# One plain feed-forward chunk instead of two at the start of each block, with the next two chunks' first products moved in between

## The chip, the cores and the metric

One core of a Trainium2 chip. The metric is the device time of one execution in microseconds (us), the median over runs. TensorE (PE in the profile) multiplies matrices and writes to eight PSUM banks; VectorE (DVE) and ScalarE (ACT) do elementwise work and read PSUM; GpSimd (POOL) issues accumulating transfers here; SyncE (SP) issues the weight loads.

## The reference

The trunk has two layers over 512 and 256 tokens of 1024 features, in float32. Each layer is feed-forward, mixer, feed-forward, so there are four feed-forward blocks, f0 to f3, each with its own weights:

```python
def swiglu_ffn(x, w1, w2):
    gate, up = jnp.split(x @ w1, 2, axis=-1)
    return (jax.nn.silu(gate) * up) @ w2
...
x = x + 0.5 * swiglu_ffn(rmsnorm(x, norm_g[li, 0]), ffn_w1[li, 0], ffn_w2[li, 0])
h = rmsnorm(x, norm_g[li, 1])
...
x = x + mix
x = x + 0.5 * swiglu_ffn(rmsnorm(x, norm_g[li, 2]), ffn_w1[li, 1], ffn_w2[li, 1])
```

The first mixer is a gated linear recurrence, the second windowed attention; a last RMSNorm closes the trunk. The hidden width is 2816, 22 chunks of 128.

## The kernel before

All 768 tokens are worked on at once, features on the partitions, tokens in two halves of 384 (half 0, half 1). Every float32 operand is split into a rounded high part and the rest (`split`: a ScalarE cast, then a VectorE subtraction), and a product is three matmuls: high x high, high x low, low x high.

**A chunk** is one 128-wide piece of the hidden layer, gate and up. It is computed in one of two ways.

- *Plain* (`up_plain`): for each half of the tokens, gate and up are each 8 blocks of 128 input features times three matmuls (L288 to L290). A plain chunk needs the activations as they are: b00 and b10 are the first and second 512 features of half 0, b01 and b11 those of half 1.
- *Seven products* (`up_pair`, matmuls on L527): gate/up and the two halves of the features form a 2 x 2 block matrix of weights, features and token halves one of activations, and seven products of sums (p1 to p7) take the place of eight. Four are of single blocks or of sums on the weights' side with b00, b10, b11 (p1, p2, p3) and the others use sums of activation blocks, t1 to t4 (p5 with t1, p6 with t2, p7 with t3, p4 with t4). The products are added up in four PSUM banks a, b, c, d; some banks are read in between: L544 copies p1 out of a before p2 is added to it, L550 copies p7 out of c before p4 is added, L556 reads p5 in d before p3 is added.

The weights' sums come in three ways: loads with an accumulating transfer on GpSimd's queue (`into`: the gate/up sum of the lower block, and `s3` for p7), and two VectorE additions (L243) before p6 and p3 in the order `UP`. Each product's weights are split into a buffer of their own (L229, L230); a plain operand takes two buffers (L186, L189). There are 8 such buffers (`WBUFS`) and 4 for unsplit loads (`RAWBUFS`). `done` gives a buffer back and `ahead` stages the next weights as far as there is room, in the order in which the products use them.

**The opening of a block.** The activations come out of the last stage token block by token block: normalised (L351), transposed on TensorE (L411, `turn`), copied (L414), split (L293, L294). Half 0 is ready first. `turn` for half 1 and `sums`, which forms t1 to t4 with four subtractions for each 512 features (L441, L442, L444, L445) and splits them, are deferred: `run_later` calls in the plain chunks issue them one by one. Before the change there are two plain chunks: both chunks' half 0, then both chunks' half 1, then the first seven-product chunks.

```python
PLAIN = 2
UP = ("p1", "p7", "p2", "p5", "p4", "p6", "p3")
```

**Groups.** Four chunks make a group of hidden activations. Their blocks are put together (`put`, `gather`, with `mix` for the sums) as operands of the seven-product down projection (`down_quad`, L608), whose results VectorE adds to x (L671). There are five groups; the last two chunks of a block go through a plain down projection.

**Order.** A framework queues the instructions of each engine, not strictly in the order of the code: one that waits may be overtaken by a later one of the same engine that does not depend on it. On the chip each queue is fixed. `issue_after` forces an order in a queue.

Of the kernel before, what the change touches and what calls it, by code (L numbers as in the profile page):

```python
# [12 lines left out]
AF = mybir.ActivationFunctionType  # L13
# [3 lines left out]
P = 128  # L17
D = 1024
DFF = 2816
NC = D // P  # L20
NF = DFF // P
# [13 lines left out]
SEQS = ((0, TA), (TA, TB))  # L35
H = T // 2
HB = H // P
PLAIN = 2
GROUPS = (NF - PLAIN) // 4
WBUFS = 8  # L40
RAWBUFS = 4
SLOTS = 21
RING = 1024
WARM = 21
UP = ("p1", "p7", "p2", "p5", "p4", "p6", "p3")
DOWN = ("p1", "p2", "p5", "p4", "p7", "p6", "p3")
FACTOR = {"p1": "b00", "p2": "b10", "p3": "b11", "p4": "t4", "p5": "t1", "p6": "t2", "p7": "t3"}


class Trunk:  # L50
# [104 lines left out]
    def load_next(self):  # L155
        key, srcs, shape, how = self.queue.pop(0)
        raws = []
        first = len(srcs) // 2 if len(srcs) == 4 else 0
        for src in srcs[first:] + srcs[:first]:
            t = self.wp.tile([P, 1024], F32, tag="wr", name=self.name("wr"), bufs=RAWBUFS)  # L160
            raw = t[:, : shape[0] * shape[1]].rearrange("p (a b) -> p a b", a=shape[0])
            if len(srcs) < 4:
                src = src.rearrange("(k p) c -> p k c", p=P)
            self.last_load = self.nc.sync.dma_start(raw, src)
            raws.append(raw)
        raws = raws[len(raws) - first :] + raws[: len(raws) - first]
        if len(raws) == 1:
            steps = self.plain_steps(key, raws[0], shape)
        else:
            steps = self.quad_steps(key, raws, srcs, how)  # L170
        self.loaded.append((len(raws), steps))

    def wtile(self):
        return self.wp.tile([P, 1024], F32R, tag="w", name=self.name("w"), bufs=WBUFS)
# [24 lines left out]
    def quad_steps(self, key, raws, srcs, order):  # L199
        nc = self.nc  # L200
        flat = lambda t: t.rearrange("p a b -> p (a b)")
        up = len(raws) == 2
        if up:
            a11, a12, a21, a22 = (flat(t[:, h : h + 4, :]) for t in raws for h in (0, 4))
            three = [srcs[1].rearrange("(k p) c -> p k c", p=P)[:, :4, :]]
        else:
            a11, a12, a21, a22 = (flat(t) for t in raws)
            three = [srcs[2][:, i : i + 1, :] for i in range(2)]
        s3 = []
        if not up:  # L210
            self.into(a21, a22)
        for i, src in enumerate(three):
            t = self.wp.tile([P, 512], F32, tag="s3", name=self.name("s3"), bufs=2)
            self.last_load = nc.sync.dma_start(t.rearrange("p (a b) -> p a b", a=src.shape[1]), src)
            self.into(t, a11[:, i * 512 : (i + 1) * 512])
            s3.append(t)
        if up:
            self.into(a21, a22)

        def split(name, srcs):  # L220
            if up:
                w = self.wtile()
                hi, lo = w[:, :512], w[:, 512:]
            else:
                hi, lo = self.wtile(), self.wtile()
            n = srcs[0].shape[-1]
            for i, src in enumerate(srcs):
                h, l = (t[:, i * n : (i + 1) * n] for t in (hi, lo))
                nc.scalar.copy(h, src)  # L229
                low = nc.vector.tensor_sub(l, src, h.bitcast(F32)).ins  # L230
            view = lambda t: t.rearrange("p (a b) -> p a b", a=4 if up else 2)
            self.staged[(*key, name)] = (view(hi), view(lo), 1 if up else 2)
            return low

        own = {"p1": [a11], "p2": [a12], "p3": [a12], "p4": [a22], "p5": [a21], "p6": [a11], "p7": s3}
        sums = {"p6": (a11, a21), "p3": (a12, a11)}
        last = [None]

        def step(name):
            if name in sums:  # L240
                into, term = sums[name]
                with self.tc.issue_after(last[0]):
                    nc.vector.tensor_add(into, into, term)  # L243
            last[0] = split(name, own[name])
            if up and name == "p5":
                self.halved = self.halved or last[0]

        return [(1 if up else 2, lambda name=name: step(name)) for name in order]
# [209 lines left out]

    xn = [None] * NBLK
    normed = mixed = first = halved = None  # L460
    normal = None
    plains = 0

    def after_block(self, b, row):
# [11 lines left out]
    def plan_ffn(self, tag, w1, w2):  # L476
        def up(i):
            gate, up = (w1[:, c * P : (c + 1) * P] for c in (i, NF + i))
            if i < PLAIN:
                self.plan((tag, i, 0), gate, (NC, P))  # L480
                self.plan((tag, i, 1), up, (NC, P))
            else:
                self.plan_quad((tag, i), (gate, up), (NC, P), UP)

        for g in range(GROUPS):
            for i in range(4 * g, 4 * g + 4):
                up(i)
            self.plan_down((tag, "down", g), w2[4 * g * P : (4 * g + 4) * P, :])
        for i in range(NF - 2, NF):
            up(i)  # L490
        for c in range(2):
            self.plan((tag, "last", c), w2[(NF - 2) * P :, c * 512 : (c + 1) * 512], (2, 512))
# [6 lines left out]
    def up_plain(self, tag, j, half):  # L499
        pss = []  # L500
        for c in range(2):
            wh, wl = self.take((tag, j, c))
            ps = self.ps(H)
            for k in range(NC):
                b = self.operand(f"b{k // 4}{half}", k % 4)
                self.mm3(ps, (wh[:, k, :], wl[:, k, :]), b, k == 0, k == NC - 1)
                if self.first:
                    self.first()
                    self.first = None
                if half == 0 and k in (((), (2, 6)), ((3, 7), (3, 7)))[j][c]:  # L510
                    self.run_later()
            if half:
                self.done((tag, j, c))
            pss.append(ps)
        t = self.tmp(H)
        with self.tc.issue_after(self.normed) if self.normed else nullcontext():
            self.nc.scalar.activation(t, pss[0], AF.Silu)
        self.normed = None
        self.nc.vector.tensor_mul(t, t, pss[1])
        return t  # L520
# [15 lines left out]
    def up_pair(self, tag, j, hold=False):  # L536
        nc = self.nc
        key = (tag, j)
        a, b, c, d = (self.ps(H) for _ in range(4))
        v, w, t = (self.tmp(H) for _ in range(3))  # L540
# [35 lines left out]
        else:  # L576
            finish()
        free("p3")
        yield w

    def down_quad(self, tag, g, hid):
# [91 lines left out]
    def ffn(self, tag, next_row):  # L673
        for g in range(GROUPS):
            hid = {}

            def put(name, src, kp):
                if name not in hid:
                    hid[name] = self.big([P, 2, 2, H], F32R)
                return self.split(src, hid[name][:, kp, 0, :], hid[name][:, kp, 1, :])  # L680

            def gather(ts, kp):
                self.mix(ts[0], ts[1], ts[2], ts[3], lambda name, src: put(name, src, kp))

            if g == 0:
                ts = {}
                for half in range(2):
                    for j in range(PLAIN):
                        t = ts[2 * j + half] = self.up_plain(tag, j, half)
                        name = f"b{j}{half}"  # L690
                        if name != "b01":
                            low = put(name, t, 0)
                        if name == "b00" and self.whole:
                            with self.tc.issue_after(low):
                                for parts in self.whole[:2]:
                                    self.nc.vector.tensor_add(*parts)
                            del self.whole[:2]
                gather(ts, 0)
                self.run_later(len(self.deferred))
            for kp in range(2):  # L700
                if g == 0 and kp == 0:
                    continue
                ts = []
                for j in range(2):
                    for half, t in enumerate(self.up_pair(tag, 4 * g + 2 * kp + j, j == 0)):
                        ts.append(t)
                        name = f"b{j}{half}"
                        if name != "b01":
                            put(name, t, kp)
                gather(ts, kp)  # L710
            self.down_quad(tag, g, hid)
# [646 lines left out]
class Unit:  # L1358
# [220 lines left out]
```

## Time and profile before

| | |
|---|---|
| median of three runs | 2731.8 us (2731.26 to 2732.34) |
| span of the profiled execution | 2730.5 us |
| outside the span, against the median | 1.3 us |
| TensorE busy | 2720.2 us, 100% |
| VectorE busy | 2110.3 us, 77% |
| ScalarE busy | 1339.0 us, 49% |
| GpSimd busy | 204.8 us, 7% |
| transfers | 293.98 MB, 108 GB/s |

The profile is of one execution, whose own total is not listed apart from its span. Engine busy times are those with at least one instruction in flight; matmuls overlap, so TensorE counts as busy although each matmul lasts 334 ns and the next starts after about half of that. A row of a group reads: line, engine, operation, output and inputs with partitions x elements, count, then busy us and mean ns of one, then idle time of the engine just before them and what ended it. In the chain, a row is start, length and what ran. In the windows a row is a stretch of the span with each engine's busy us and its instructions in brackets, the granted TensorE clock, the share of the transfer engines, and GB/s. In a timeline a row is start, length, engine, line, operation, count.

### The profile page before, as it was taken

Reading aid. Unit: us, or ns where it says so; the run is one execution under the profiler, and the core shown is the slowest. Engines: PE = TensorE matmul, PEld = TensorE weight load, DVE = VectorE, ACT = ScalarE, POOL = GpSimd, SP = SyncE. Lnnn points to the kernel's source line nnn. Section 1 sums busy time; section 2 is a strip of 40 time slices with the busy share of each in tenths; the row PEclk is TensorE's granted clock in tenths of the full one; section 3 lists DMA queues with packets and bytes.
Section 4 is the critical chain, followed back from the end, with each engine's and each line's share of the span. In section 5 each row is a group of like instructions: output and inputs, shape, how many; then the busy total and the mean of one; then the engine's idle time right before and its main releaser. Section 6 shows DMA issues by size and latency. Waiting matters only on the chain.

```text
span 2730.5 us, 44549 instructions
## 1 busy us (share of the span) xinstructions
PE 2720.2 (100%) x17305; PEld 2483.8 (91%) x17305; DVE 2110.3 (77%) x3789; ACT 1339.0 (49%) x2507; POOL 204.8 (7%) x243
## 2 busy tenths in 40 slices
PE   9999999999999999999999999999999999999998
PEld 9999999889888889999999999999987789999998
DVE  8888788567476778778888878887847768787877
ACT  6444444456466554444446444444546754444443
POOL 1110110000000000111110011101000000111000
PEclk9999999999999999999999999999999999999999
DMA  6544554311110524465553355544422123555443
GB/s 183 136 123 117 127 143 120 123 56 48 55 41 25 143 65 120 113 147 129 128 121 102 88 129 139 135 116 112 133 72 78 47 62 87 130 139 135 117 112 108
DMA packets 331411, 293.98 MB, mean 108 GB/s; under 512 B 11752, under 2 KB 258240, under 8 KB 331200
## 3 DMA queue, kind: packets, MB, share of 16 engines
q1 hardware_dynamic: 294352, 212.89, 26.6%
q0 software_dynamic: 32544, 64.76, 13.6%
q10 hardware_dynamic: 4304, 13.49, 1.4%
q8 instruction: 135, 2.21, 0.3%
q14 instruction: 76, 0.62, 0.1%
HBM read 216.91 MB, written 9.44 MB: 83 GB/s over the span
## 4 chain that ended last, share of the span: by engine, by line
PE 97%; DVE 1%; ACT 1%; issue 0%; DMA 0%; DVEq 0%; SPq 0%; ACTq 0%
PE ps L527 42%; PE ps L608 21%; PE ps L288 9%; PE ps L289 9%; PE ps L290 9%; PE ps L856 1%; PE ps L643 1%; PE ps L1451 1%; PE ps L1442 1%; PE ps L1004 1%; PE ps L1390 1%; PE ps L411 1%; PE ps L980 0%; PE ps L969 0%; DVE x L671 0%
## 5 line engine op out<-in xcount | busy, mean ns | idle before, releaser
L527 PE MATMUL ps<-big,w 128*128 128x384 f32 x6720 | 1169.7, 334 | 0.6 <-ACT tA L544 0.6
L527 PEld LDWEIGHTS ps<-big,w 128*128 128x128 f32 x6720 | 1165.9, 188 | 2.8 <-ACT tA L544 1.2
L229 ACT CAST w<-wr 128x512 fp32r<-128x512 f32 (+1 forms) x606 | 424.2, 710 | 721.8 <-DVE wr L243 305.4
L230 DVE TENSOR_TENSOR w<-wr,w 128x512 fp32r<-128x512 f32 (+1 forms) x606 | 480.5, 798 | 225.4 <-ACT w L229 158.5
L608 PE MATMUL ps<-w,big 128*128 128x512 f32 x2520 | 575.4, 389 | 0.0
L608 PEld LDWEIGHTS ps<-w,big 128*128 128x128 f32 x2520 | 472.8, 188 | 97.5 <-DVE x L671 0.3
L671 DVE SCALAR_TENSOR_TENSOR x<-ps,x 128x512 f32<-128x512 f32 x468 | 302.6, 681 | 4.7 <-PE ps L290 4.7
L288 PE MATMUL ps<-w,big 128*128 128x512 f32 x576 | 232.5, 404 | 0.0
L290 PE MATMUL ps<-w,big 128*128 128x512 f32 x576 | 225.5, 391 | 0.0
L289 PE MATMUL ps<-w,big 128*128 128x512 f32 x576 | 225.1, 391 | 0.0
L288 PE MATMUL ps<-big,w 128*128 128x384 f32 (+2 forms) x640 | 217.9, 342 | 0.2
L289 PE MATMUL ps<-big,w 128*128 128x384 f32 (+2 forms) x640 | 215.8, 337 | 0.4 <-DVE big L371 0.2
L290 PE MATMUL ps<-big,w 128*128 128x384 f32 (+2 forms) x640 | 215.1, 336 | 0.0
L293 ACT CAST big<-tA 128x384 fp32r<-128x384 f32 x296 | 147.8, 512 | 117.5 <-DVE tA L572 40.4
L153 POOL DMA_DIRECT2D s<-wr x122 | 106.3, 913 | 1300.1 <-DMA wr<-in_ffn_w_dram 623.6
L189 DVE TENSOR_TENSOR w<-wr,w 128x1024 fp32r<-128x1024 f32 (+1 forms) x88 | 105.9, 1209 | 82.0 <-ACT w L186 73.4
L294 DVE TENSOR_TENSOR big<-tA,big 128x384 fp32r<-128x384 f32 x296 | 159.9, 551 | 8.2 <-ACT big L293 7.8
L153 POOL DMA_DIRECT2D wr<-wr x101 | 87.6, 868 | 1009.3 <-DVE tA L1110 386.0
L186 ACT CAST w<-wr 128x1024 fp32r<-128x1024 f32 (+1 forms) x90 | 93.0, 1035 | 93.4 <-PE ps L289 66.3
L288 PEld LDWEIGHTS ps<-w,big 128*128 128x128 f32 x576 | 108.3, 188 | 25.6 <-issue 4.6
L290 PEld LDWEIGHTS ps<-w,big 128*128 128x128 f32 x576 | 108.1, 188 | 23.5 <-issue 0.4
L289 PEld LDWEIGHTS ps<-big,w 128*128 128x128 f32 x640 | 121.0, 189 | 9.4 <-DVE big L294 1.0
(191 smaller groups left out, 2891.8 us busy)
## 6 DMA issues: line engine op xcount, KB each, us to landing
wr<-in_ffn_w_dram SPq DMA_DIRECT2D x264, 512.0 KB, 3.9
s<-wr POOLq DMA_DIRECT2D x122, 256.0 KB, 5.1
s<-in_ffn_w_dram SPq DMA_DIRECT2D x120, 256.0 KB, 3.3
wr<-wr POOLq DMA_DIRECT2D x80, 256.0 KB, 4.2
wr<-in_hg_w_in_dram SPq DMA_DIRECT2D x40, 512.0 KB, 3.8
wr<-wr POOLq DMA_DIRECT2D x21, 512.0 KB, 6.0
spill<-x ACTq DMA_DIRECT2D x12, 512.0 KB, 2.9
x<-spill ACTq DMA_DIRECT2D x12, 512.0 KB, 3.3
```

What stands on the lines that cost most here:

```text
L153: self.nc.gpsimd.dma_start(out, src, accum_op=ALU.add)
L189: eng.tensor_sub(lo, raw[:, ks, :], hi.bitcast(F32))
L229: nc.scalar.copy(h, src)
L230: low = nc.vector.tensor_sub(l, src, h.bitcast(F32)).ins
L288: nc.tensor.matmul(out, a[0], b[0], start=first, stop=False)
L289: nc.tensor.matmul(out, a[0], b[1], start=False, stop=False)
L290: nc.tensor.matmul(out, a[1], b[0], start=False, stop=last)
L293: self.nc.scalar.copy(hi, src)
L294: return self.nc.vector.tensor_sub(lo, src, hi.bitcast(F32)).ins
L527: self.nc.tensor.matmul(ps, a[x], b[y], start=first and k == 0 and i == 0, stop=k == 3 and i == 2, skip_group_check=True,)
L608: nc.tensor.matmul(ps, a[x], w[y], start=name == chain and kp == 0 and q == 0, stop=kp == 1 and q == 2, skip_group_check=True,)
L671: return self.nc.vector.scalar_tensor_tensor(x, ps, c, x, ALU.mult, ALU.add).ins
```

## The change

One chunk per block is plain, not two. Chunks 1 and 2 are now of the seven-product kind, in a new function `open_pair` whose weights are ordered by `OPEN`. Chunk 0's half 0 is followed by p1 and p2 of chunk 1 and of chunk 2, which need only half 0; then come chunk 0's half 1, p3 of both, p5 of both, and then the rest of chunk 1 (p7, p4, p6) and of chunk 2. Chunk 3 follows in `up_pair` as before. The deferred steps for half 1 are issued behind the same number of matmuls as before. The first gather of four blocks now takes place behind chunk 1's products. In `OPEN` both VectorE additions of a chunk's weights come before p3.

```diff
-PLAIN = 2
-GROUPS = (NF - PLAIN) // 4
+GROUPS = (NF - 2) // 4
...
+OPEN = ("p1", "p2", "p3", "p5", "p7", "p4", "p6")
@@ load_next
-        self.loaded.append((len(raws), steps))
+        if how is not OPEN:
+            self.loaded.append((len(raws), steps))
+        elif self.opened is None:
+            self.loaded.append((2, steps[:2]))
+            self.opened = steps[2:]
+        else:
+            a, b = self.opened, steps[2:]
+            self.loaded.append((0, steps[:2]))
+            self.loaded.append((2, [a[0], b[0], a[1], b[1]] + a[2:]))
+            self.loaded.append((2, b[2:]))
+            self.opened = None
@@ quad_steps
-        sums = {"p6": (a11, a21), "p3": (a12, a11)}
+        sums = {"p6": [(a11, a21)], "p3": [(a12, a11)]}
+        if order is OPEN:
+            sums = {"p3": sums["p6"] + sums["p3"]}
...
-            if name in sums:
-                into, term = sums[name]
+            for into, term in sums.get(name, ()):
@@ plan_ffn
-            if i < PLAIN:
+            if i == 0:
...
-                self.plan_quad((tag, i), (gate, up), (NC, P), UP)
+                self.plan_quad((tag, i), (gate, up), (NC, P), OPEN if i < 3 else UP)
@@ up_plain
-                if half == 0 and k in (((), (2, 6)), ((3, 7), (3, 7)))[j][c]:
+                if half == 0 and c and k in (2, 6):
                     self.run_later()
@@ new
+    def open_pair(self, tag, j, hold):
...
+        p("p1", a, True, False)
+        nc.scalar.copy(v, a)
+        free("p1")
+        self.run_later()
+        p("p2", a, False, True)
+        nc.scalar.activation(a, a, AF.Silu)
+        free("p2")
+        self.run_later()
+        yield
+        d = self.ps(H)
+        p("p3", d, True, False)
+        nc.scalar.copy(w, d)
+        free("p3")
+        yield
+        p("p5", d, False, True)
+        free("p5")
+        yield
+        c, b = self.ps(H), self.ps(H)
+        p("p7", c, True, False)
+        nc.vector.tensor_add(w, w, c)
+        free("p7")
+        p("p4", c, False, True)
+        nc.vector.tensor_sub(w, w, d)
+        free("p4")
+        p("p6", b, True, True)
+        t = self.tmp(H)
+        nc.vector.tensor_sub(v, v, b)
+        nc.vector.tensor_sub(t, c, v)
+        nc.vector.tensor_mul(t, t, a)
+        free("p6")
+        yield t
+        nc.vector.tensor_sub(w, w, v)
+        nc.vector.tensor_add(v, v, d)
...
@@ ffn
             if g == 0:
-                ts = {}
-                for half in range(2):
-                    for j in range(PLAIN):
-                        t = ts[2 * j + half] = self.up_plain(tag, j, half)
...
-                gather(ts, 0)
+                first = [self.up_plain(tag, 0, 0)]
+                low = put("b00", first[0], 0)
...
+                for j in (1, 2):
+                    pairs[j] = self.open_pair(tag, j, j == 2)
+                    next(pairs[j])
+                first.append(self.up_plain(tag, 0, 1))
                 self.run_later(len(self.deferred))
+                for _ in range(2):
+                    for j in (1, 2):
+                        next(pairs[j])
+                pairs[0] = first
```

More of the change, by code (lines that the diff above doesn't have):

```diff
@@ L460 @@
     normed = mixed = first = halved = None
-    normal = None
+    normal = opened = None
     plains = 0
@@ L578, in up_pair, with finish @@
         free("p3")
+        yield w
+    def open_pair(self, tag, j, hold):
+        nc = self.nc
+        key = (tag, j)
+        a, d, c, b = self.ps(H), None, None, None
+        v, w = (self.tmp(H) for _ in range(2))
+        p = lambda name, ps, first, last: self.product(key, name, FACTOR[name], ps, first, last)
+        free = lambda *names: [self.done((*key, name)) for name in names]
+        p("p1", a, True, False)
[31 more added lines that the diff above has]
+        nc.vector.tensor_add(v, v, d)
+        def finish(after=None):
+            with self.tc.issue_after(after) if after else nullcontext():
+                self.last_act = nc.scalar.activation(v, v, AF.Silu).ins
+            self.last_dve = nc.vector.tensor_mul(w, v, w).ins
+        if hold:
+            self.tail = finish
+        else:
+            finish()
         yield w
@@ L683, in gather @@
                 self.mix(ts[0], ts[1], ts[2], ts[3], lambda name, src: put(name, src, kp))
+            pairs = {}
             if g == 0:
-                ts = {}
-                for half in range(2):
-                    for j in range(PLAIN):
-                        t = ts[2 * j + half] = self.up_plain(tag, j, half)
[L690 to L697, printed above, removed]
-                gather(ts, 0)
+                first = [self.up_plain(tag, 0, 0)]
+                low = put("b00", first[0], 0)
+                if self.whole:
+                    with self.tc.issue_after(low):
+                        for parts in self.whole[:2]:
+                            self.nc.vector.tensor_add(*parts)
+                    del self.whole[:2]
+                for j in (1, 2):
+                    pairs[j] = self.open_pair(tag, j, j == 2)
+                    next(pairs[j])
+                first.append(self.up_plain(tag, 0, 1))
                 self.run_later(len(self.deferred))
+                for _ in range(2):
+                    for j in (1, 2):
+                        next(pairs[j])
+                pairs[0] = first
             for kp in range(2):
-                if g == 0 and kp == 0:
-                    continue
                 ts = []
                 for j in range(2):
-                    for half, t in enumerate(self.up_pair(tag, 4 * g + 2 * kp + j, j == 0)):
+                    n = 4 * g + 2 * kp + j
+                    for half, t in enumerate(pairs.get(n) or self.up_pair(tag, n, j == 0)):
                         ts.append(t)
                         name = f"b{j}{half}"
-                        if name != "b01":
+                        if name != "b01" and (n or half):
                             put(name, t, kp)
```

## The prediction

> **What bounds the kernel now.** I read the page first: busy times, the clock row, the chain that ended last. Then the groups by shape, the chain in order of time, and the windows and timelines of the four openings of a feed-forward block (f0 to f3), the only places that the diff touches.
>
> ```profile
> span 2730.5 us, 44549 instructions
> ...
> PE 2720.2 (100%) x17305; PEld 2483.8 (91%) x17305; DVE 2110.3 (77%) x3789; ACT 1339.0 (49%) x2507; POOL 204.8 (7%) x243
> ...
> PEclk9999999999999999999999999999999999999999
> ...
> PE 97%; DVE 1%; ACT 1%; issue 0%; DMA 0%; DVEq 0%; SPq 0%; ACTq 0%
> ```
>
> TensorE is the bound: it carries 97% of the chain, and only 10.3 us of the span have no matmul in flight. The median of the runs, 2731.8, is 1.3 us above the profiled span. What lies outside the span stays as it is, so the sum is a difference taken off 2731.8. Anything between 2726.3 and 2737.3 (0.2%) I call no change.
>
> ```profile
> 48.51 29.12 PE ps L527 x168
> ...
> 1031.07 29.12 PE ps L527 x168
> 1060.19 28.60 PE ps L608 x126
> 1088.79 58.26 PE ps L527 x336
> ...
> 1521.03 29.12 PE ps L527 x168
> ...
> 2272.23 29.12 PE ps L527 x168
> ```
>
> These pieces of the chain give the pace: 58.26/336 = 0.1734 us per matmul of 384 columns, without a hole. The four x168 pieces are the first two seven-product chunks of f0, f1, f2 and f3. Their starts, which I call S, are 48.51, 1031.07, 1521.03 and 2272.23.
>
> **The change part by part.**
>
> *Matmuls.* A plain chunk is 2 halves x 2 (gate, up) x 8 k x 3 = 96 matmuls, a seven-product chunk 7 x 4 x 3 = 84. One chunk per block changes kind: 12 x 0.1734 = 2.08 us less TensorE work per block, 8.32 us in four, with as many weight loads less. All of it is on the path, so the best case is 2731.8 - 8.3 = 2723.5.
>
> *Order.* After 48 plain matmuls on half 0 come p1, p2 of both chunks (48), the plain half 1 (48), p3 of both (24), p5 of both (24), then p7. So p7, the first user of t3, starts at S exactly as the old first p1 did. But p5 needs t1 24 matmuls (4.16 us) before S, and its weights and p3's must be staged 4.2 to 8.3 us before S, where formerly the first split chunk needed nothing before S.
>
> *VectorE work.*
>
> ```profile
> L230 DVE TENSOR_TENSOR w<-wr,w 128x512 fp32r<-128x512 f32 x480 | 326.7, 686 | 148.2 <-ACT w L229 142.5
> L189 DVE TENSOR_TENSOR w<-wr,w 128x1024 fp32r<-128x1024 f32 x86 | 104.6, 1221 | 82.0 <-ACT w L186 73.4 <-PE ps L527 7.5
> L243 DVE TENSOR_TENSOR wr<-wr,wr 128x512 f32<-128x512 f32 x80 | 54.6, 683 | 0.0
> L556 DVE TENSOR_TENSOR tA<-tA,ps 128x384 f32<-128x384 f32 x80 | 44.1, 551 | 26.6 <-PE ps L527 26.5
> L544 ACT COPY tA<-ps 128x384 f32<-128x384 f32 x80 | 38.4, 479 | 59.7 <-PE ps L527 59.4
> ```
> ```profile
> 28.61 1.89 DVE L590 TENSOR_TENSOR x<-x,x 128x512 f32<-128x512 f32 x3
> ...
> 46.32 0.68 DVE L230 TENSOR_TENSOR w<-wr,w 128x512 fp32r<-128x512 f32 x1
> 46.92 0.68 DVE L230 TENSOR_TENSOR w<-s,w 128x512 fp32r<-128x512 f32 x1
> 47.52 2.69 DVE L294 TENSOR_TENSOR big<-big,big 128x768 fp32r<-128x768 f32 x3
> 50.13 0.55 DVE L294 TENSOR_TENSOR big<-tA,big 128x384 fp32r<-128x384 f32 x1
> 50.60 1.29 DVE L230 TENSOR_TENSOR w<-wr,w 128x512 fp32r<-128x512 f32 x2
> ```
>
> Back to back, VectorE starts a 512-wide weight operation every 0.60 us (46.32 to 46.92), a 768-wide one every (50.13 - 47.52)/3 = 0.87, a 384-wide one every 0.47 (50.13 to 50.60). Per block the change adds 7 splits and 2 sums of weights (9 x 0.60 = 5.4) and 7 operations on products (3.3); it removes two 1024-wide weight splits (about 1.2 each) and two multiplications (0.94). Net +5.4 us, while the time in which to do it shrinks by 2.08.
>
> ```profile
> core 0: us, PE busy (x) PEld busy (x) DVE busy (x) ACT busy (x) POOL busy (x), PEclk, DMA share, GB/s
> 15.67:33.90 18.23, 18.23 (x114) 17.99 (x114) 16.95 (x26) 14.32 (x26) 6.34 (x7) 1.00 1.11 254
> 33.90:50.13 16.23, 16.23 (x96) 16.23 (x95) 15.65 (x20) 10.07 (x16) 0.86 (x1) 1.00 0.21 45
> 50.13:77.63 27.50, 27.50 (x160) 27.50 (x159) 24.30 (x44) 14.88 (x26) 2.62 (x3) 1.00 0.50 125
> 994.27:1008.83 14.56, 14.47 (x92) 13.83 (x91) 11.37 (x14) 14.54 (x25) 1.72 (x2) 1.00 0.46 109
> 1008.83:1026.01 17.18, 17.18 (x101) 17.18 (x100) 17.06 (x24) 10.57 (x18) 0.00 (x0) 1.00 0.05 16
> 1031.07:1060.19 29.12, 29.12 (x170) 29.12 (x169) 21.59 (x36) 14.54 (x25) 2.63 (x3) 1.00 0.42 109
> 1498.78:1515.29 16.51, 16.51 (x97) 16.51 (x96) 16.51 (x23) 10.59 (x18) 0.00 (x0) 1.00 0.05 17
> 2249.99:2267.16 17.17, 17.17 (x101) 17.17 (x100) 17.05 (x23) 10.57 (x18) 0.00 (x0) 1.00 0.05 16
> ```
>
> The rows 33.90:50.13, 1008.83:1026.01, 1498.78:1515.29 and 2249.99:2267.16 run from the first subtraction of the sums (t1 to t4 of both halves of the first 1024 features) to their last split. In each VectorE is full. These ends lie 5.06, 5.74 and 5.07 us before S in f1, f2, f3, and 1.62 us *behind* S in f0, where the normalisation of the first tokens starts everything later.
>
> *f1 to f3.* The sums are 16 operations of 0.87 = 13.9 us. What else must be through before p7 can finish: the first plain product's multiplication and split and the second's multiplication (1.4), five weight splits (two p3, two p5, one p7: 3.0), and p3's four sums (2.4). Together 20.7 us from 1008.83, so 1029.5, 1.5 us before S; 3.9 before if the four sums go into the 3.2 us in which VectorE was idle in 994.27:1008.83. The p3 splits are due 6 to 8 us before S: the old sums held 3.3 us of foreign operations between their own, so there is room. I take a stall of 0 here; ends 0 and 2.1.
>
> *f0.* Again 13.9, with p3's sums and splits (2 x 1.8), two p5 and one p7 (1.8) and one multiplication (0.47). The first p3's 1.8 can take the place of the three x21 subtractions at 28.61, which nobody needs before the down products at 77.63. That leaves 18.0 from 33.90: 51.9 for the last split (t2), 51.0 for the one before (t3). p7's second half is due at S + 1.04 = 49.55: 1.5 us late. If the first p3 also comes behind 33.90 it is 3.3; if p6's first half (6 matmuls, 1.04) fills the hole, 0.4. I take 1.5.
>
> *Behind S.* In f1 VectorE has 7.5 us idle from S to the down products, in f0 3.2. In f0 what does not fit (about 1 us) eats into the down weights staged ahead; a down product lasts 28.60/7 = 4.09 us, so a delay of 1 us is hidden. Cost 0, upper end 2.
>
> *Banks read between two products.* p2 adds to the bank from which p1's copy (L544) has yet to be read, and p4 to the one that w's addition (as L556) reads; before, another product always lay between, now none does in the code. p3 and p5 are covered by the other chunk's.
>
> ```profile
> PE ps L527 <- ACT tA L544: 0.6, 1, 0.6
> ```
> ```profile
> 998.30 0.34 PE L290 MATMUL ps<-big,w 128*128 128x384 f32 x1
> 998.48 0.93 PE L411 MATMUL ps<-ident_r,big 128*128 128x128 f32 x7
> ```
> ```profile
> 1000.31 1.83 DVE L294 TENSOR_TENSOR big<-big,big 128x768 fp32r<-128x768 f32 x2
> ```
>
> The first row is the one time that TensorE waited for that copy: 0.6 us. The others show that the queue's order isn't the code's: TensorE had run 24 matmuls of the plain chunk by 998.48, before b10 was split (1000.31). In the code gate's 13th matmul needs b10, so the 24 are the b00 halves of gate and up, and transposes of the other half fill on. In the same way p1 of the other chunk can go between p1 and p2, and p6 between p7 and p4. I charge one uncovered turnaround in all, 0.6; ends 0 and 16 x 0.6 = 9.6. The Trainium skill ("TensorE: Matmul & The Clock Gate", "Step-by-step: what each phase is for") says that only weight loads are pulled ahead and matmuls stay in the order in which they were queued; by that rule alone nothing on the chip fills such a wait, and the sum would come out at the upper end. Whether it is paid hangs on the order that was queued, and these rows speak for a filled one.
>
> *Others.* ScalarE gets 7 casts, 2 copies and 2 Silu for 2 casts and 2 Silu; outside its full stretch 994.27:1008.83 it has a third idle: 0, up to 1. SP and POOL: one more load (256 KB) and two accumulating transfers per block, at a DMA share of 0.05 to 0.5; in f0 (1.11 until 33.90) they come 20 us before use: 0, up to 1. The third chunk's loads go out some 15 us later, and still some 15 us ahead of use: 0.
>
> *Sum.* -8.3 + 1.5 (f0) + 0.6 = -6.2: 2725.6.
>
> **The rivals.** (A) The forecast, f0 losing most of its gain, 2724.5 to 2727.5. (B) All four blocks gain: 2723.5. For: the filled holes above; against: f0's sums end behind S already. (C) Slower: the turnarounds aren't filled, and p4's wait on VectorE stands behind the sums in its queue. Per opening 2 x 0.6 for ScalarE and 2 x (0.6 + 1.3, half of a batch of three splits, 2.6) = 5.0, against 2.08: +2.9 x 4, 2743.5. It decides from 2.08 us per opening, and shows as slower from 3.45. For: VectorE full in all four rows; against: the reordering. (D) VectorE is late in all openings: p3's sums, asked for ahead of t1 to t4, push these back by 1.5 to 2.1 us beyond my count, and the gain is gone: 2729.5 to 2732. Against: 1.5 to 3.9 us of slack in f1 to f3. (E) f0's stall is long enough to lower TensorE's clock: at half pace the 36 matmuls of p7, p4 and p6 cost 6.2 more, 2731.8. The clock row shows no such fall anywhere. The same page (its Part 1) has the clock halve after an idle window of about 3.4 us; no hole of that length between matmuls is in the quoted rows.
>
> **How the numbers follow.** A 0.44, B 0.19, D 0.20, E 0.04, C 0.13. Faster: B and all but 0.04 of A, 0.59; same: that 0.04, D and E, 0.28; slower: C, 0.13. The range runs from B's 2723.0 (half a microsecond of scatter) to D's end, 2731.5; C and a corner of D lie outside. A alone: 2724.5 to 2727.5.
>
> **What would show it.** 384 matmuls fewer in the 384-column groups of L288 to L290, 336 more in L527's; the stretch from the first plain matmul to the first down product shorter by 2.1 us in f1 to f3, and by 0 to 1.5 in f0, with TensorE waiting there for the split of t3 or for p7's weights. Wrong if TensorE waits for L544's successor or for w's addition in every opening (C), or for L230 in f1 to f3 (D).

## The result, and the profile after

| | before | after |
|---|---|---|
| median | 2732.1 us (2731.3 to 2733.5) | 2761.3 us (2759.5 to 2762.0) |
| ratio | | 1.0105 [1.0091, 1.0119] |
| span of the profiled execution | 2730.5 us | 2760.0 us |
| TensorE busy | 2720.2 us | 2724.4 us |
| time without a matmul in flight | 10.3 us | 35.6 us |

The change makes the kernel 29 us slower, 1.1%. The page of the kernel after, with the span, the busy times, the chain by engine and the costliest group:

```profile
span 2760.0 us, 44576 instructions
...
PE 2724.4 (99%) x17257; PEld 2481.1 (90%) x17257; DVE 2131.2 (77%) x3845; ACT 1349.3 (49%) x2535; POOL 211.1 (8%) x251
...
PE 92%; DVE 3%; DMA 2%; ACT 2%; issue 1%; POOL 0%; DVEq 0%; SPq 0%; ACTq 0%; POOLq 0%
...
L538 PE MATMUL ps<-big,w 128*128 128x384 f32 x7056 | 1238.8, 335 | 19.9 <-DVE tA L618 17.7
```

There are 48 matmuls fewer (17257 for 17305), as the change says, 8.3 us at 0.1734 us each. Yet TensorE is busy 4.2 us longer, and its share of the chain fell from 97% to 92%. Both halves of the loss are to be explained: 25.3 us more idle, and busy time that is 12.5 us above what 48 matmuls fewer should have left (4.2 up where 8.3 down was due). A stretch in which no matmul is in flight is called a hole below.

Line numbers moved by about ten: the product matmul L527 is now L538, the weight cast and split L229 and L230 are L239 and L240, the weights' sum L243 is L254, the operand split L294 is L305, the down product L608 is L671 and its addition to x L734. L618 is new, `w += c` in `open_pair`: it reads p7 out of bank c before p4 may add to it. The list of TensorE's waits (total, times, longest) names the place:

```profile
PE ps L538 <- DVE tA L618: 17.7, 5, 6.7
PE ps L300 <- DVE big L305: 4.7, 3, 4.2
...
PE ps L538 <- DVE big L305: 0.5, 1, 0.5
```

p4 waits for L618 in every block, 17.7 us in all. The chain in order of time tells the blocks apart; these rows start the second group behind each opening, first before, then after:

```profile
193.24 58.26 PE ps L527 x336
...
1175.66 58.26 PE ps L527 x336
...
1665.62 58.26 PE ps L527 x336
...
2416.82 58.26 PE ps L527 x336
```
```profile
208.80 58.26 PE ps L538 x336
...
1194.66 58.26 PE ps L538 x336
...
1690.07 58.26 PE ps L538 x336
...
2446.27 58.26 PE ps L538 x336
```

The lead of before grows by 15.6 us in f0, 3.4 in f1, 5.5 in f2 and 5.0 in f3, together 29.5, the whole difference of the spans. Behind the openings the pace is the old one, 58.26 us for 336.

**Where f1's 3.1 us hole comes from.** Timelines of f1, each row with the idle time before it and what ended it; first the load of chunk 3's weights and its accumulating transfer before the change, then the way from that load to TensorE after it:

```profile
997.05 2.11 SPq L164 DMA_DIRECT2D wr<-in_ffn_w_dram  x2
...
1001.63 0.86 POOL L153 DMA_DIRECT2D s<-wr  x1 [17.33 <-DMA wr<-in_ffn_w_dram]
```
```profile
1043.86 3.19 SPq L164 DMA_DIRECT2D wr<-in_ffn_w_dram  x4
...
1048.59 0.89 POOL L153 DMA_DIRECT2D s<-wr  x1 [48.60 <-DMA wr<-in_ffn_w_dram]
...
1054.36 0.62 ACT L239 CAST w<-s 128x512 fp32r<-128x512 f32 x1 [5.71 <-DMA s<-wr]
...
1055.01 0.69 DVE L240 TENSOR_TENSOR w<-s,w 128x512 fp32r<-128x512 f32 x1 [4.21 <-ACT w L239]
...
1060.51 0.54 DVE L618 TENSOR_TENSOR tA<-tA,ps 128x384 f32<-128x384 f32 x1
...
1061.11 2.20 PE L538 MATMUL ps<-big,w 128*128 128x384 f32 x11 [3.09 <-DVE tA L618]
```

Chunks 1 and 2 are now both in work from before half 1 until their last product, and hold all four raw buffers. Chunk 3's loads go out at 1043.86, where before they had gone out at 997.05: 46.8 us later, or 31 without the 15.6 us that f0 had lost by then. GpSimd then adds to s, ScalarE waits 5.71 us for that transfer, VectorE 4.21 us for ScalarE. The transfer itself landed 5.6 us after its issue, and four weight loads had gone out in the 5 us before it; before the change the same transfer took 3.3 us (in f2 and f3 it took 6.5 and 6.7 us, for 4.4 and 4.2). In VectorE's fixed queue chunk 3's splits stand ahead of chunk 2's L618 (1060.51), so a product of chunk 2 waits for weights of chunk 3. Chunk 3's own first product comes only behind this hole, 17 us after its loads went out. The 3.09 us are what TensorE could not fill.

**f0's other hole.** Two pieces of the chain, and then timelines of f0:

```profile
21.25 7.41 DMA s<-wr
61.46 8.12 DMA s<-wr
```
```profile
28.74 0.69 DVE L254 TENSOR_TENSOR wr<-wr,wr 128x512 f32<-128x512 f32 x1 [4.85 <-DMA s<-wr]
...
32.76 1.82 DVE L305 TENSOR_TENSOR big<-big,big 128x768 fp32r<-128x768 f32 x2
...
33.77 0.69 PE L300 MATMUL ps<-big,w 128*128 128x384 f32 x1 [4.23 <-DVE big L305]
```

p3's sum now comes first and adds into a11, in place. The accumulating transfer issued at 21.25 still reads a11, until 28.66. VectorE stands there for 4.85 us with the split of b01 (32.76) behind it, and TensorE stands for 4.23. The second piece (61.46) is chunk 3's late s, as in f1, and makes the 6.7 us hole.

**What a hole costs besides itself.** The granted clock is the share of full speed at which TensorE may run. Four microseconds behind each of the five longest holes (windows: TensorE busy and matmuls, then the granted clock):

```profile
1061.11:1065.11 4.00, 4.00 (x23) 1.00 0.35 114
1554.91:1558.91 4.00, 4.00 (x15) 0.63 0.33 123
2312.43:2316.43 4.00, 4.00 (x15) 0.60 0.34 116
72.66:76.66 4.00, 4.00 (x13) 0.52 0.63 128
33.77:37.77 4.00, 4.00 (x13) 0.50 0.01 1
```

Behind four of the five the clock was about half, and 13 or 15 matmuls ran where 23 run at full clock. That is 8 + 8 + 10 + 10 = 36 matmuls, 6.2 us: half of the 12.5 us of busy time. One of the four half-clock stretches runs on behind its window. Counted over the whole trace from the starts of consecutive matmuls, each against the usual distance for its shape (173 ns for 384 columns), the half clock cost 7.4 us. The same count puts the other 5 us into pauses that do not show as idle: a wait counts as idle only once the last matmul, 334 ns long, has ended, and a pause shorter than that leaves TensorE busy.

### The profile page after: what moved, and what is told of

The parts are those of the page before. It is cut to its first block, busy times and chain, and to the rows that moved or that the text cites. A ratio compares the mean times of both kernels' runs of the same rounds, so it can differ in the third digit from the quotient of the medians.

```text
span 2760.0 us, 44576 instructions
## 1 busy us (share of the span) xinstructions
PE 2724.4 (99%) x17257; PEld 2481.1 (90%) x17257; DVE 2131.2 (77%) x3845; ACT 1349.3 (49%) x2535; POOL 211.1 (8%) x251
## 4 chain that ended last, share of the span: by engine, by line
PE 92%; DVE 3%; DMA 2%; ACT 2%; issue 1%; POOL 0%; DVEq 0%; SPq 0%; ACTq 0%; POOLq 0%
PE ps L538 41%; PE ps L671 20%; PE ps L299 8%; PE ps L300 8%; PE ps L301 8%; PE ps L921 1%; DMA s<-wr 1%; PE ps L706 1%; PE ps L1516 1%; PE ps L1507 1%; DMA wr<-in_ffn_w_dram 1%; PE ps L1069 1%; PE ps L1455 1%; DVE w L240 1%; ACT w L239 0%
## 5 line engine op out<-in xcount | busy, mean ns | idle before, releaser
L538 PE MATMUL ps<-big,w 128*128 128x384 f32 x7056 | 1238.8, 335 | 19.9 <-DVE tA L618 17.7
L538 PEld LDWEIGHTS ps<-big,w 128*128 128x128 f32 x7056 | 1228.1, 188 | 27.2 <-DVE tA L618 19.6
L239 ACT CAST w<-wr 128x512 fp32r<-128x512 f32 (+1 forms) x630 | 439.2, 707 | 708.6 <-DVE wr L254 317.0
L240 DVE TENSOR_TENSOR w<-wr,w 128x512 fp32r<-128x512 f32 (+1 forms) x630 | 496.0, 793 | 217.6 <-ACT w L239 153.8
L671 PE MATMUL ps<-w,big 128*128 128x512 f32 x2520 | 576.5, 389 | 0.8 <-DVE x L734 0.8
L671 PEld LDWEIGHTS ps<-w,big 128*128 128x128 f32 x2520 | 472.4, 188 | 99.4 <-ACT big L304 1.4
L734 DVE SCALAR_TENSOR_TENSOR x<-ps,x 128x512 f32<-128x512 f32 x468 | 302.6, 681 | 4.8 <-PE ps L301 4.7
L300 PE MATMUL ps<-big,w 128*128 128x256 f32 (+2 forms) x512 | 174.0, 340 | 5.1 <-DVE big L305 4.7
L299 PE MATMUL ps<-big,w 128*128 128x256 f32 (+2 forms) x512 | 175.7, 346 | 0.1
L301 PE MATMUL ps<-big,w 128*128 128x256 f32 (+2 forms) x512 | 173.0, 338 | 0.0
L305 DVE TENSOR_TENSOR big<-tA,big 128x384 fp32r<-128x384 f32 x296 | 159.7, 551 | 6.7 <-ACT big L304 6.5
L199 DVE TENSOR_TENSOR w<-wr,w 128x1024 fp32r<-128x1024 f32 (+1 forms) x80 | 96.2, 1208 | 81.7 <-ACT w L196 73.4
L299 PEld LDWEIGHTS ps<-w,big 128*128 128x128 f32 x576 | 108.3, 188 | 25.7 <-issue 4.6
L196 ACT CAST w<-wr 128x1024 fp32r<-128x1024 f32 (+1 forms) x82 | 84.5, 1034 | 92.0 <-PE ps L300 66.3
L301 PEld LDWEIGHTS ps<-w,big 128*128 128x128 f32 x576 | 108.1, 188 | 23.6 <-issue 0.4
L300 PEld LDWEIGHTS ps<-w,big 128*128 128x128 f32 x576 | 108.4, 188 | 19.6
```

The source lines that it names most:

```text
L199: eng.tensor_sub(lo, raw[:, ks, :], hi.bitcast(F32))
L299: nc.tensor.matmul(out, a[0], b[0], start=first, stop=False)
L300: nc.tensor.matmul(out, a[0], b[1], start=False, stop=False)
L301: nc.tensor.matmul(out, a[1], b[0], start=False, stop=last)
L305: return self.nc.vector.tensor_sub(lo, src, hi.bitcast(F32)).ins
L538: self.nc.tensor.matmul(ps, a[x], b[y], start=first and k == 0 and i == 0, stop=k == 3 and i == 2, skip_group_check=True,)
```

## The experiments

Theories. L: chunk 3's weights arrive too late, since its loads wait for raw buffers. Q: the arrival is harmless by itself, and only the order of VectorE's queue makes p4 wait. W: in f0 the in-place sum of p3 waits for the accumulating transfer. All medians stand beside the kernel before on the same chip (2732.2 to 2732.6).

**Chunk 3's staging behind chunk 2's L618 (for Q).**

```diff
+        if self.held + ... > WBUFS or (self.shut and self.loaded[0][1] is self.third):
...
+        with self.tc.issue_after(self.behind) if steps is self.third and self.behind else nullcontext():
+            go()
@@ open_pair
+        summed = nc.vector.tensor_add(w, w, c).ins
+        if hold:
+            self.shut, self.behind = False, summed
```

> The splits of chunk 3's weights are queued on VectorE behind the addition of chunk 2's p7 to w, which p4 waits for; loads, buffers and products stay as in the changed kernel. Theory Q (queue order): in the changed kernel VectorE stood before chunk 3's p7 weights, whose accumulating transfer had not landed, and so delayed an addition that TensorE was waiting for. Expected by Q: the four waits of TensorE on that addition (6.7, 3.1, 3.7 and 4.0 us, 17.7 in all with a short one) go, with the half-clock stretch that followed the longest (about 2 us) and small waits behind it: 2761.3 - 20 = 2738 to 2743; a wait of about 4 us in f0's first half stays. Rival L (the loads themselves come too late for TensorE): the wait only moves to chunk 3's p1 or p7, less than a third is won, 2754 or more. Rival B (VectorE has too much work): the waits shrink by less than half, 2750 to 2758.

Measured: 2753.3 us, 1.0075 [1.0060, 1.0090], 8 us better than the change. TensorE's waits:

```profile
PE ps L542 <- DVE w L242: 5.0, 5, 3.2
PE ps L303 <- DVE big L308: 4.2, 3, 3.8
PE ps L542 <- ACT w L241: 2.2, 3, 1.0
PE ps L677 <- DVE w L242: 2.1, 1, 2.1
```

The wait on L618 is gone, and TensorE's products wait for their weights themselves (L241, L242) instead; the last row is the same for a down product. Q's 2738 to 2743 is missed by 10 us. The queue's order was the place of the wait and a part of its size; the late weights stay.

**p3's sums in another order (for W): a12 += a11, then a12 += a21, so that a11 is not written before p6.**

```diff
-            sums = {"p3": sums["p6"] + sums["p3"]}
+            sums["p3"].append((a12, a21))
```

> p3's weights in the opening chunks are summed as a12 += a11, then a12 += a21, so that a11 isn't overwritten before p6; one VectorE addition more per chunk. Theory W: in f0 the in-place sum into a11 had to wait until the accumulating transfer that reads a11 had landed (7.4 us behind a transfer of x on GpSimd's queue), and VectorE stood before it with the split of b01 behind; TensorE then waited 4.2 us and ran at a granted clock of 0.5 for 4.9 us. Expected by W: f0 shorter by 4.2 + 2.4 = 6.6, the rest as it was or up to 1 longer: 2754 to 2757. Rival: f0's first half waits because VectorE is simply full; then no gain, 2760 to 2763.

Measured: 2764.6 us, 1.0117 [1.0100, 1.0134]: a miss, 3 us worse. A timeline of f0 and the waits:

```profile
27.98 0.62 ACT L239 CAST w<-wr 128x512 fp32r<-128x512 f32 x1 [3.65 <-DVE wr L254]
...
29.13 0.55 PE L422 MATMUL ps<-ident_r,big 128*128 128x128 f32 x3 [2.07 <-ACT big L425]
```
```profile
PE ps L538 <- DVE tA L618: 19.3, 4, 5.8
```

The 4.2 us hole went, but p3's cast in ScalarE's queue still waited 3.65 us for the sums, ahead of the turned operands' copies. In f1 to f3 the holes at L618 were 2.7, 1.3 and 0.8 us longer than in the change, and the transfer of s ahead of them took 3.3, 1.0 and 0.6 us longer from issue to landing (8.9, 7.5 and 7.3 us). Why it did is not shown.

**Both together.**

> e1's queue order and e2's order of sums together. Q and W: their gains add up, 20 + 6.6 us: 2733 to 2737, no stretch at half clock left in f0, the blocks f1 to f3 within 1 us of the kernel before. If my count of the freed matmuls were the whole of it, all four blocks would be 2.1 us shorter than before, 2724; I expect f0 to keep 3 to 5 us of short waits, as its sums end behind the first use. Rival L: 2745 or more.

Measured: 2758.4 us, 1.0092 [1.0077, 1.0108], worse than the first alone. Neither edit makes the weights arrive earlier.

**Chunk 3's load left out (for L): it splits chunk 2's buffers.**

```diff
+        again = key[1] == 3 and how is UP
+        if again:
+            raws = self.kept
+        for src in () if again else srcs[first:] + srcs[:first]:
```

> Chunk 3 of each block takes the weights that chunk 2 left in its load buffers, so its loads and its accumulating transfers are left out (its results are those of other weights); everything else, the queue order of the splits too as far as the planner keeps it, as in the changed kernel. Theories Q and L both have the late transfer as the cause: TensorE's waits on w's addition go, 2737 to 2744. Rival T (p7 and p4 next to each other in one bank, with VectorE's own work as the delay): the waits stay at 3 us or more each, 2755 or more. Against e1 it tells how much of the loss is the transfer itself: Q says that e1 gains as much as this one to within 3 us, L that this one gains at least 10 us more.

Measured: 2739.5 us, 1.0025 [1.0016, 1.0035], 21.8 us better than the change. The largest wait that is left:

```profile
PE ps L310 <- DVE big L315: 4.3, 3, 3.8
```

No wait on L618 remains, with chunk 3's splits still ahead of it in VectorE's queue. f0 keeps W's hole. By the starts of the second groups all four blocks gain, 8.2, 3.2, 6.0 and 5.1 us. L against Q is decided by this: with the weights there, the order does no harm. The run has no late transfer because it has none for chunk 3 at all, so what the transfers cost by running beside others is not told apart here.

**Chunk 3's raw halves early, everything computed: six raw buffers, paid for with an arena slot and a tA tile; and the kernel before with that slot and tile taken away.**

```diff
-RAWBUFS = 4
-SLOTS = 21
+RAWBUFS = 6
+SLOTS = 20
...
-("tA", 8, TA)
+("tA", 7, TA)
```

> The changed kernel with six raw weight buffers in place of four, paid for with one of 21 arena slots and one of 8 tA tiles. The third chunk's two loads no longer wait for buffers that the first two chunks hold, and all transfers and sums stay. Theory L (the third chunk's loads go out too late): the waits on the adding of c behind VectorE's weight splits go from all four blocks, about 22 us are saved as when the third chunk was not loaded at all, and the time is 2737 to 2743, the first block keeping some 7 us. Rival T (the transfers and accumulations of the third chunk disturb wherever they stand, so that leaving them out helped and moving them does not): 2750 or more. Rival B (the slot and the tile taken away cost more than the loads give): waits on arena slots or tA tiles in TensorE's list, time above 2745.

> The kernel before with the 20 arena slots and 7 tA tiles of the previous run, and its own four raw buffers: what the missing slot and tile cost by themselves. If they cost nothing: 2732 within 1.5 us. Rival B: 2736 or more.

Measured: 2753.8 us, 1.0078 [1.0066, 1.0091], and for the kernel before 2738.1, 1.0021 [1.0012, 1.0030]. The slot and tile cost 5.7 us by themselves, so the earlier raw halves bring 7.5 + 5.7 = 13 us of the 22, if the price is the same in the changed kernel. The time itself lies outside L's range and inside T's. A timeline of f1 shows the rest:

```profile
1037.97 0.37 SPq L224 DMA_DIRECT2D s<-in_ffn_w_dram  x1
...
1041.61 0.87 POOL L153 DMA_DIRECT2D s<-wr  x1 [43.58 <-DVE w L240]
...
1047.84 0.62 ACT L239 CAST w<-s 128x512 fp32r<-128x512 f32 x1 [3.93 <-DMA s<-wr]
...
1049.70 24.37 PE L538 MATMUL ps<-big,w 128*128 128x384 f32 x139 [1.48 <-DVE tA L618]
```

s has two buffers of its own, which chunks 1 and 2 hold as well: s was loaded late all the same (1037.97; 1041.6, named in the next expectation, is its addition). The hole shrank from 3.09 to 1.48 us. In all four blocks the waits on L618 fell from 17.7 to 8.8 us, with all transfers in place. That speaks against T, that the transfers do harm wherever they stand, but does not exclude it for the rest: no run here brings all of chunk 3's weights early.

**First half and s early, second half late: a fifth raw buffer, a third for s, for one arena slot.**

```diff
+            if third and len(raws) == 1:
+                self.add_three(s3, ...)
...
-SLOTS = 21
+SLOTS = 20
...
-name=self.name("wr"), bufs=RAWBUFS)
+name=self.name("wr"), bufs=RAWBUFS + 1)
...
-name=self.name("s3"), bufs=2)
+name=self.name("s3"), bufs=3)
```

> The changed kernel with a fifth raw buffer and a third buffer for s (one of 21 arena slots given for them, tA keeps 8), and the third chunk's queue order set to: first raw half, s, second raw half. In the run with six raw buffers the raw halves went out early, but s still waited for one of its two buffers (its load at 1041.6 us in the second block). Here s and the first half go out early too, and only the second half, needed four products later, is late. Theory L (late arrival of the third chunk, s included): the waits on the adding of c that were left (8.8 us in four, and the half clock behind the first) go, 7 to 10 us less than with six raw buffers: 2743 to 2747, of which 5.7 us is the price of the missing slot. Rival (the order of VectorE's queue, not the arrival, makes that wait): 2751 or more, waits on the adding still over 5 us.

Measured: 2759.1 us, 1.0100 [1.0086, 1.0114]: a miss, 5 us worse than with both halves early. `add_three` loads s and adds a11 to it, here ahead of the second half's load. A timeline of f1:

```profile
1053.78 1.14 ACT L247 CAST w<-wr 128x512 fp32r<-128x512 f32 x2 [5.46 <-DMA wr<-wr]
...
1054.43 0.69 DVE L248 TENSOR_TENSOR w<-wr,w 128x512 fp32r<-128x512 f32 x1 [4.93 <-ACT w L247]
...
1058.57 16.93 PE L546 MATMUL ps<-big,w 128*128 128x384 f32 x96 [2.52 <-DVE tA L626]
```

s is no longer waited for. Now p5's weights, which need the second half and its accumulating transfer (wr<-wr), hold up the same queues. "Needed four products later" was wrong for the queues: the splits stand there far ahead of their products. By its signs the rival came (above 2751, and 8.3 us of waits on the addition), though ahead of the addition there stands a late transfer once more.

**f0's p3 staging behind the split of half 1's operands (for W), alone and with the two early loads.**

```diff
-            if self.held + self.loaded[0][1][0][0] > WBUFS:
+            if self.held + self.loaded[0][1][0][0] > WBUFS or self.loaded[0][1] is self.thirds:
...
+        if feeds_ffn and self.thirds and half and part:
+            self.turned, self.thirds = low, None
+            self.ahead()
```

> The changed kernel, but in the first block alone the staging of p3's weights of chunks 1 and 2 (sums and splits) is kept behind the split of the second half's turned operands. Theory W (VectorE, standing at the first sum for the accumulating transfer that reads its target, holds up the split that TensorE needs): the 4.2 us wait in half 1 of the plain chunk goes, with it 15 matmuls at half clock (2.5 us); the second wait of the first block (6.7 us, the late load) stays. Saved 5 to 7 us: 2754 to 2757. Rival (the wait only moves to another instruction of the same queues, as it did when the sums were reordered): 2759 or more.

> Both together: six raw buffers with a slot and a tile less, and the first block's p3 staging behind the operand splits. If L and W are the whole of the loss, what is left is the kernel before less 8.3 us of matmuls plus about 2 us a block of short waits and switches: 2731 to 2736. Rival: losses overlap less than they seem, a third wait takes their place in the first block: 2738 or more.

> The same with the first block's p3 staging behind the operand splits. If the two losses are separate, another 5 to 7 us go: 2737 to 2742, so 2731 to 2736 without the price of the missing slot. Rival: 2745 or more, the first block's products then waiting on p3's weights instead.

Measured: 2754.7 us, 1.0083 [1.0070, 1.0097], 6.6 us better than the change. TensorE's waits for operand splits (L309), first of the products, then of the plain chunk, where the change has 4.7 us:

```profile
PE ps L545 <- DVE big L309: 1.6, 3, 0.9
...
PE ps L304 <- DVE big L309: 0.5, 2, 0.2
```

W is borne out, but for less than 6.6 us. By the starts of the second groups, f0 gained 4.3 us (204.47 for 208.80), and 2.4 us came in f2, which the edit does not touch: there the hole was 2.55 us long and the clock stayed at 1.00, where the change had 3.68 us and half clock. With six raw buffers 2749.7, 1.0065 [1.0053, 1.0078], 4.1 us better than without the gate; with the third s 2751.8, 1.0069 [1.0057, 1.0082], 7.3 better. The two totals were expected 14 to 19 and 10 to 15 us lower: the expectations took L to be cured there, and the first of them left out the price of the missing slot.

**The kernel before with one arena slot less.**

```diff
-SLOTS = 21
+SLOTS = 20
```

> The kernel before with 20 arena slots in place of 21 and nothing else. Its down products took 391 ns each in place of 389 with a slot and a tA tile less, with no wait behind that. If it is the slot (where operands lie in the memory): 2737 to 2739 and 391 ns again. If it is the tA tile: 2732 to 2734.

Measured: 2737.1 us, 1.0018 [1.0009, 1.0027]. The groups of the down products, before and with the slot gone:

```profile
L608 PE MATMUL ps<-w,big 128*128 128x512 f32 x2520 | 575.4, 389 | 0.0
```
```profile
L608 PE MATMUL ps<-w,big 128*128 128x512 f32 x2520 | 579.8, 390 | 0.3 <-DVE x L671 0.3
```

It is the slot: 4.4 us more in these matmuls, with 0.3 us of waiting.

**Chunk 3's load left out and f0's gate: L and W both away.**

> The changed kernel with 21 slots, the third chunk's loads and accumulations left out (it takes the second chunk's buffers) and the first block's p3 staging behind the operand splits: what the change is worth with both losses away. 2739.5 less 5 to 7 us: 2732.5 to 2735, the 8.3 us of matmuls then being eaten by short waits and switches of about 2 us a block. If the saving of matmuls comes through: 2726 to 2729. If the gate brings nothing here: 2738 or more.

Measured: 2735.1 us, 1.0011 [1.0002, 1.0020], the span 2734.0. The page's busy times and the waits:

```profile
PE 2717.5 (99%) x17257; PEld 2474.9 (91%) x17257; DVE 2131.2 (78%) x3845; ACT 1349.0 (49%) x2535; POOL 204.3 (7%) x243
```
```profile
PE ps L555 <- DVE tA L584: 1.9, 2, 1.7
PE ps L555 <- DVE big L319: 1.6, 3, 0.9
PE ps L555 <- DVE w L253: 1.2, 2, 0.8
```

26.2 of the 29.2 us are back, but not the 8.3 us of matmuls. By the starts of the second groups (196.80, 1178.43, 1667.95, 2420.46), f1 and f2 are 0.8 and 0.4 us shorter than before, f0 is 3.6 and f3 1.3 us longer. Against before, TensorE has 6.2 us more without a matmul (16.5 for 10.3: many short waits, about half of them by time in f0, and one of 1.7 us for L584 in f3), and its busy time fell by 2.7 us, not 8.3. There is no half clock in these openings. Counted from the starts of the matmuls, as above, the other 5.6 us are pauses that do not show as idle, about 3 us at the waits themselves and about 3 us in pauses shorter than a matmul. The openings are cut into more short runs of matmuls, but no run measured by itself whether that makes the short pauses. None of these kernels was faster than the one before.

## Why the prediction was wrong

*The step that failed* is the term "The third chunk's loads go out some 15 us later, and still some 15 us ahead of use: 0". It asked how far the loads go out ahead of the product that uses them, and that half of it held: in f1 they were 17 us ahead of chunk 3's first product. What counts is the place of their splits in ScalarE's and VectorE's queues, which is ahead of chunk 2's L618. And they were not 15 us later but 31 in f1. The term measured 21.8 us, by the run without those loads and transfers.

*f0's transfers* ("they come 20 us before use: 0, up to 1") failed in the same way. Their product was indeed far off, but the transfer reads a11, which p3's sum overwrites: 6.6 us by the gate, 4.3 of them in f0, and 4.4 us between the two runs without chunk 3's loads.

*The stall of 1.5 us for the sums in f0* is there, but small beside this. TensorE's waits for the splits of t1 to t4 were 0.5 us in the changed kernel and 1.6 us with L and W away, about as foretold.

*The matmuls* were counted rightly, 48 fewer, and so was VectorE's work (20.9 us more in four blocks, 5.2 a block, for 5.4). But the 8.3 us never came off the path in full: with both late arrivals away the kernel was still 2.9 us slower than before. What ate them, 6.2 us of short waits and about 6 us of pauses that do not show as idle, stood in the sum as 1.5 + 0.6.

*Rival C* named the place rightly (p4 waits for w's addition, which stands behind something else in VectorE's queue) and its time, 2743.5, was the nearest, and its sign, a wait for w's addition in every opening, came; but with the wrong cause ahead of it: not the sums t1 to t4 but chunk 3's weight splits. Its other half, p2 waiting for p1's copy, did not come: the queue put other products between them, as the prediction argued, and TensorE's list of waits has no row for that copy in `open_pair` (L600).

*Rival E*'s mechanism came, in four places and for other holes than the one it named: 6.2 us in the windows shown, which equals its price only by chance, and 7.4 in all. The prediction gave it 0.04, since the trace of before had no hole of that length; holes of that length were what had to be priced. The page's clock row, on which it also leaned, cannot show such a fall: each of its 40 slices is 69 us long, and the row of the kernel after reads 9 throughout as well.

*The range* was set by the bounds of the terms, and the two terms that failed had a bound of 0 and of 1. VectorE's 77% and "ahead of use" hid that a transfer's latency (7.41 and 8.12 us above) stands in front of queues that cannot be overtaken.

## What to carry to other kernels

When a change keeps two work items open at once instead of one, count every buffer that they hold (raw, sums, splits) and ask whose load waits for it. Judge a late load not by the product that needs it but by the first instruction in any fixed queue that waits for it, and by all that stands behind that instruction. Treat an in-place sum as a wait for every transfer that still reads its target.

## What the runs showed of the hardware

*The clock falls after short holes, if they lie badly.* By the clock records of the traces the granted clock is 1.00 or 0.50 and changes on a grid. In the changed kernel the half clock begins at 32.12, 69.66, 1554.46 and 2312.22 us, which are 11, 435 and 222 steps of 3.413 us apart, and lasts one step or two; the other runs show the same step. The hole of 3.09 us in f1 lies across two steps in the changed kernel, and in one step in the run with f0's gate alone. Two steps of the first and then of the second (TensorE busy and matmuls, then the granted clock):

```profile
1056.12:1059.53 3.41, 1.90 (x11) 1.00 0.64 150
1059.53:1062.94 3.41, 1.83 (x10) 1.00 0.00 0
```
```profile
1052.84:1056.25 3.41, 0.32 (x2) 1.00 0.07 28
1056.25:1059.66 3.41, 3.41 (x12) 0.50 0.30 82
```

In the step ahead of each fall from full clock TensorE was busy for at most 1.93 of 3.41 us. The border is not sharp in this measure, since steps with 1.53 (f1 of the run with s early), 1.83 and 1.90 us were followed by full clock. So the length of a hole alone does not decide. Holes of 2.11, 2.33, 2.45 and 2.52 us left the clock at 1.00, while behind holes of 2.07 us (f0 of the run with the sums in another order) and 2.12 us (f0 of the run with chunk 3's staging behind L618) it fell to 0.50. Of two holes of 2.55 us one left it at 1.00 (f2 with f0's gate alone) and one did not (f0 of the run with s early). Behind the hole of 2.85 us and every longer one, but for that of 3.09 us in the changed kernel, it was 0.50 within 2 us. With both orders together, two holes of 0.92 and 0.56 us in one step were enough.

The Trainium skill ("TensorE: Matmul & The Clock Gate", Part 1) speaks of a free-running idle window of about 3.4 us at whose end the clock halves. The grid agrees with a free-running window of that length; that the window has to be idle does not agree with these runs.

*A buffer less can slow matmuls that never wait.* One arena slot less cost 5.0 us, 4.4 of them in the down products. That their operands then lie in other places is the likely reason, but neither the places nor which of them are slow was looked at.
